# An encoder layer's down projection: 30 of its 64 row pairs as seven products of sums of blocks

## The chip, the cores and the metric

The kernel runs on one core of one Trainium2 chip. The metric is device microseconds (us) of one execution; lower is better. TensorE (PE) multiplies, VectorE (DVE), ScalarE (ACT) and GpSimd (POOL) work elementwise, and SyncE (SP), ACT and POOL issue transfers (DMAs).

## The reference, cut to what matters

One layer with 256 tokens, 2048 channels and everything in float32: an input projection, two kinds of attention, a gated merge, an output projection, and then an MLP. The change is in the last product of the MLP, `u` (256 x 8192) times `w_down` (8192 x 2048).

```python
proj = h @ w_in                       # 256x2048 by 2048x10240: q, k, v of both attentions, gates
mixed = g_a * (oa @ w_branch_a) + g_b * (on @ w_branch_b)
x = x + rms_norm(mixed @ w_out, norm_mix_post)
h = rms_norm(x, norm_mlp_pre)
u = square(relu(h @ w_up))            # 256x2048 by 2048x8192
x = x + rms_norm(u @ w_down, norm_mlp_post)
```

## The kernel before, in words

**Precision.** TensorE takes float32 at a rounded precision (`fp32r`). Each operand is therefore split in two parts: ACT casts it to `fp32r` (hi, L116), DVE subtracts that from the original (lo, L117), and a product is three matmuls: hi by hi, hi by lo, lo by hi. Every matmul of interest has a stationary operand of 128x128 and a moving one of 128x512.

**Weights.** All weights come from HBM on SP's queue into three buffers of 1 MB (pool `wp`, tag `raw`), and from there into three buffers each of hi and lo. A load on SP waits until DVE has done with the buffer of three loads earlier, and a cast on ACT waits until TensorE has done with the hi buffer of three casts earlier.

**Stages.** Projections and attention come first. Then come the gates, the branch products and the merge, in groups 1024 columns wide (`wide_group`, L671). The output projection follows (`agroup`, L221), then the up projection (`wgroup`, L184), and last the down projection, written out at L951 to L1015. In the up projection each of 16 column groups has 4 chunks of weights. Its result goes through `u_evac` (L955) into a page `u`, 128 channels by 4 blocks by 256 tokens, and all 16 pages stay in SBUF.

**The down projection before.** A loop over 64 blocks of 128 rows of `w_down`: each loads a row block whole (128x2048), splits it, and runs 24 matmuls (`dmm`, L968): 2 token halves by 4 column blocks of 512, by 3. The eight PSUM banks hold all 8 sums for the whole stage. The hi and lo of `u` are made as they are needed (`usplit`, L939). The last 3 row blocks are ordered so that one bank after the other is finished. For each, ACT squares and sums the bank (L1003) and DVE multiplies it by the gain (L1005). Per token half, DVE then adds up the sums (L1007), POOL takes the power -0.5 (L89), four DVE instructions scale and add the residual (L1012), and SP writes 4 pieces out (L1015).

**Seven products.** The gate groups already have what the change uses. A pair of row blocks k, k+1 by 1024 columns is a 2x2 block product with the 2 token halves. The plain way (`Products.eight`, L656) is 8 block products, 24 matmuls, into 4 banks. The other way (`Products.seven`, L644) is 7 block products of sums of blocks, 21 matmuls, into banks 0 to 6. At the end of a group `combine` (L662) makes the four results of them in 5 instructions. `pair_weights` (L602) prepares the weights. For a plain pair that is one cast and one subtraction of 2048 elements. For a pair of seven it is three additions (L614 to L616), a cast and a subtraction of 1536 elements (L613, L617), and two casts and two subtractions of 1024 (L622, L623). Their results lie in a pool of five buffers, of which a pair takes four. Bank 7 and banks 1 to 3 also take the plain pairs, so both kinds add up in the same group (`MIXED`, L728).

**Order.** The program's instructions are put in order per engine when it is built, by a scheduler that follows its own timeline; at run time each engine takes its instructions strictly in that order. Each transfer on SP or ACT also takes one of eight completion counters by turns, and waits until the transfer that had the counter before it is done.

Of the kernel before, what the change touches and what calls it, by code (L numbers as in the profile page):

```python
# [17 lines left out]
P = 128  # L18
# [20 lines left out]
def encoder_layer(ctx: ExitStack, tc: tile.TileContext, a, out):  # L39
# [897 lines left out]
    ust = {}  # L937

    def usplit(i):  # L939
        uh = page([P, 4, T], F32R, f"uh{i}")  # L940
        ul = page([P, 4, T], F32R, f"ul{i}")
        nc.scalar.copy(uh, uT[i])
        nc.vector.tensor_sub(ul, uT[i], uh.bitcast(F32))
        ust[i] = (uh, ul)

    def dweight(k):
        if k % 4 == 0 and k // 4 not in ust:
            usplit(k // 4)
        return weight(a["w_down"], k, 1, 0, D, f"d{k}")

    uT = []  # L951
    for cg in range(DFF // 512):
# [8 lines left out]
        uT.append(u)  # L961
        if cg == DFF // 512 - 2:
            usplit(0)

    acc = [[bank(f"acc{t}{c}", t * 4 + c >= 8 - NMM) for c in range(4)] for t in range(2)]
    NK = DFF // P
    LAST = 3
    def dmm(k, t, c, w):  # L968
        uh, ul = ust[k // 4]
        ts_ = slice(t * P, (t + 1) * P)  # L970
        cs = slice(c * 512, (c + 1) * 512)
        hi, lo = w
        nc.tensor.matmul(acc[t][c], uh[:, k % 4, ts_], hi[:, 0, cs], start=(k == 0), stop=False)  # L973
        nc.tensor.matmul(acc[t][c], uh[:, k % 4, ts_], lo[:, 0, cs], start=False, stop=False)  # L974
        nc.tensor.matmul(  # L975
            acc[t][c], ul[:, k % 4, ts_], hi[:, 0, cs], start=False, stop=(k == NK - 1)
        )

    ws = [dweight(k) for k in range(2)]
    for t in range(2):  # L980
        for k in range(2):
            for c in range(4):
                dmm(k, t, c, ws[k])
    for k in range(2, NK - LAST):
        w = dweight(k)
        for t in range(2):
            for c in range(4):
                dmm(k, t, c, w)

# [5 lines left out]
    ws = [dweight(k) for k in range(NK - LAST, NK)]
    for t in range(2):
        ssd = small(4, f"ssd{t}")
        zw = [page([P, 1024], F32, f"zw{t}{h}") for h in range(2)]
# [70 lines left out]
```

## Time and profile before

| what | value |
|---|---|
| median of 3 runs | 1386.31 us (1385.98 to 1386.63) |
| profiled execution | 1386.53 us, of which the span of the profile is 1384.7 us |
| PE busy | 1363.7 us (98% of the span) |
| DVE busy | 851.7 us (62%) |
| ACT busy | 659.6 us (48%) |
| POOL busy | 7.9 us (1%) |
| transfers | 265.11 MB, mean 191 GB/s |
| up projection, down projection | about 700 to 1027 us, 1027 to 1376 us of the span |

A row of a group of instructions has line, engine, operation, output and inputs with their shapes, the count, then busy time, mean ns of one, and the idle time of the engine just before them with what ended it. Rows of the timeline begin with the start and the duration in us. Rows of a table of windows have the window, its length, then busy us and count of PE, of weight loads (PEld), DVE, ACT and POOL, the clock that TensorE was granted, the share of the transfer engines' time, and GB/s.

### The profile page before, as it was taken

Reading aid. Unit: us, or ns where it says so; the run is one execution under the profiler, and the core shown is the slowest. Engines: PE = TensorE matmul, PEld = TensorE weight load, DVE = VectorE, ACT = ScalarE, POOL = GpSimd, SP = SyncE. Lnnn points to the kernel's source line nnn. Section 1 sums busy time; section 2 is a strip of 40 time slices with the busy share of each in tenths; the row PEclk is TensorE's granted clock in tenths of the full one; section 3 lists DMA queues with packets and bytes.
Section 4 is the critical chain, followed back from the end, with each engine's and each line's share of the span. In section 5 each row is a group of like instructions: output and inputs, shape, how many; then the busy total and the mean of one; then the engine's idle time right before and its main releaser. Section 6 shows DMA issues by size and latency. Waiting matters only on the chain.

```text
span 1384.7 us, 16956 instructions
## 1 busy us (share of the span) xinstructions
PE 1363.7 (98%) x6861; PEld 1157.6 (84%) x6861; DVE 851.7 (62%) x1093; ACT 659.6 (48%) x923; POOL 7.9 (1%) x19
## 2 busy tenths in 40 slices
PE   7999999999999999999899999999999999999997
PEld 6888888888888888888788888888888888888886
DVE  6878866677857876654755554555566554444445
ACT  7455455544643544443754444444465443333332
POOL 0000000000000000000000000000000000000000
PEclk9999999999999999999999999999999999999999
DMA  8675745564655565766456565556555556555551
GB/s 292 204 230 165 205 153 182 178 180 156 206 187 184 208 223 172 248 225 195 127 178 212 161 205 184 196 189 192 182 183 208 186 191 235 183 196 199 186 200 71
DMA packets 105198, 265.11 MB, mean 191 GB/s; under 512 B 15008, under 2 KB 16288, under 8 KB 96928
## 3 DMA queue, kind: packets, MB, share of 16 engines
q1 hardware_dynamic: 104976, 264.03, 58.2%
q8 instruction: 53, 0.87, 0.3%
q14 instruction: 25, 0.20, 0.0%
q10 hardware_dynamic: 144, 0.01, 0.0%
HBM read 261.92 MB, written 3.92 MB: 192 GB/s over the span
## 4 chain that ended last, share of the span: by engine, by line
PE 98%; DVE 1%; DMA 0%; ACT 0%; SPq 0%; issue 0%; DVEq 0%; POOLq 0%; POOL 0%; ACTq 0%
PE u_p L192 17%; PE u_p L193 9%; PE acc L975 8%; PE acc L974 8%; PE acc L973 8%; PE qa_p L192 2%; PE ka_p L192 2%; PE qn_p L192 2%; PE kn_p L192 2%; PE ga L639 2%; PE y_p L232 2%; PE y_p L231 2%; PE ga L642 2%; PE ga L641 2%; PE y_p L230 2%; PE gb L642 2%
## 5 line engine op out<-in xcount | busy, mean ns | idle before, releaser
L192 PE MATMUL u_p<-h2T,u_h 128*128 128x512 f32 x1024 | 359.3, 397 | 1.0 <-DVE h2T L870 1.0
L193 PE MATMUL u_p<-h2T,u_l 128*128 128x256 f32 x1024 | 284.1, 280 | 0.0
L117 DVE TENSOR_TENSOR d_l<-d_w,d_h 128x1024 fp32r<-128x1024 f32 x128 | 151.1, 1222 | 164.1 <-ACT d_h L116 163.7
L117 DVE TENSOR_TENSOR u_l<-u_w,u_h 128x1024 fp32r<-128x1024 f32 x128 | 151.1, 1222 | 145.1 <-ACT u_h L116 143.8
L192 PEld LDWEIGHTS u_p<-h2T,u_h 128*128 128x128 f32 x1024 | 191.7, 188 | 45.7 <-DVE h2T L870 1.2
L116 ACT CAST d_h<-d_w 128x1024 fp32r<-128x1024 f32 x128 | 127.9, 1047 | 191.5 <-PE acc L975 187.9
L974 PE MATMUL acc<-d_l,uh 128*128 128x512 f32 x512 | 199.0, 389 | 0.0
L975 PE MATMUL acc<-d_h,ul 128*128 128x512 f32 x512 | 198.9, 389 | 0.0
L973 PE MATMUL acc<-d_h,uh 128*128 128x512 f32 x512 | 198.2, 389 | 0.0
L193 PEld LDWEIGHTS u_p<-h2T,u_l 128*128 128x128 f32 x1024 | 193.5, 189 | 1.3
L116 ACT CAST u_h<-u_w 128x1024 fp32r<-128x1024 f32 x128 | 128.0, 1048 | 123.1 <-PE u_p L192 62.3
L974 PEld LDWEIGHTS acc<-d_l,uh 128*128 128x128 f32 x512 | 96.1, 188 | 20.1
L973 PEld LDWEIGHTS acc<-d_h,uh 128*128 128x128 f32 x512 | 96.1, 188 | 19.9
L975 PEld LDWEIGHTS acc<-d_h,ul 128*128 128x128 f32 x512 | 96.1, 188 | 19.8
L117 DVE TENSOR_TENSOR y_l<-y_w,y_h 128x1024 fp32r<-128x1024 f32 x32 | 37.9, 1222 | 30.9 <-ACT y_h L116 30.9
L116 ACT CAST y_h<-y_w 128x1024 fp32r<-128x1024 f32 x32 | 32.0, 1047 | 40.9 <-PE y_p L232 32.6
L230 PE MATMUL y_p<-y_h,mh 128*128 128x512 f32 x128 | 50.1, 391 | 0.0
L231 PE MATMUL y_p<-y_l,mh 128*128 128x512 f32 x128 | 49.9, 390 | 0.0
L232 PE MATMUL y_p<-y_h,ml 128*128 128x512 f32 x128 | 49.8, 390 | 0.0
L192 PE MATMUL qa_p<-hT,qa_h 128*128 128x512 f32 x128 | 47.7, 419 | 1.2 <-DVE hT L275 1.2
L192 PE MATMUL qn_p<-hT,qn_h 128*128 128x512 f32 x128 | 45.9, 400 | 0.0
L192 PE MATMUL kn_p<-hT,kn_h 128*128 128x512 f32 x128 | 45.4, 398 | 0.0
(549 smaller groups left out, 2378.3 us busy)
## 6 DMA issues: line engine op xcount, KB each, us to landing
u_w<-in_w_up SPq DMA_DIRECT2D x64, 1024.0 KB, 5.4
d_w<-in_w_down SPq DMA_DIRECT2D x64, 1024.0 KB, 5.0
y_w<-in_w_out SPq DMA_DIRECT2D x16, 1024.0 KB, 5.3
ka_w<-in_w_in SPq DMA_DIRECT2D x8, 1024.0 KB, 6.7
va_w<-in_w_in SPq DMA_DIRECT2D x8, 1024.0 KB, 5.2
qn_w<-in_w_in SPq DMA_DIRECT2D x8, 1024.0 KB, 5.1
kn_w<-in_w_in SPq DMA_DIRECT2D x8, 1024.0 KB, 5.1
vn_w<-in_w_in SPq DMA_DIRECT2D x8, 1024.0 KB, 5.1
```

The source lines that it names most:

```text
L116: nc.scalar.copy(hi[part], raw[part])
L117: nc.vector.tensor_sub(lo[part], raw[part], hi[part].bitcast(F32))
L192: nc.tensor.matmul(ps[b], hi[:, k % 4, cs], mv, start=(k == 0), stop=False)
L193: nc.tensor.matmul(ps[b][:, :T], lo[:, k % 4, cs], mv[:, :T], start=False, stop=(k == nk - 1))
L230: nc.tensor.matmul(ps[t], sh, hi[:, k % 4], start=(k == 0), stop=False)
L231: nc.tensor.matmul(ps[t], sh, lo[:, k % 4], start=False, stop=False)
L232: nc.tensor.matmul(ps[t], sl, hi[:, k % 4], start=False, stop=(k == nk - 1))
L639: nc.tensor.matmul(self.ps[i], sh, wh[:, blk], start=i not in self.begun, stop=False)
L642: nc.tensor.matmul(self.ps[i], sl, wh[:, blk], start=False, stop=last)
L973: nc.tensor.matmul(acc[t][c], uh[:, k % 4, ts_], hi[:, 0, cs], start=(k == 0), stop=False)
L974: nc.tensor.matmul(acc[t][c], uh[:, k % 4, ts_], lo[:, 0, cs], start=False, stop=False)
L975: nc.tensor.matmul(acc[t][c], ul[:, k % 4, ts_], hi[:, 0, cs], start=False, stop=(k == NK - 1))
```

## The change: what it does

The down projection becomes two halves of 1024 output columns (`g`), each a group like those of the gates with all eight banks. A half runs through 32 pairs of row blocks. A column group of the up projection (`cg`) gives 4 row blocks, that is 2 pairs, and two groups (an even one and the odd one after it) make a block of 4 pairs. The pairs of even groups are done by seven products, those of odd groups plainly, alternating. In the first block of each half three of the four are plain. So there are 15 pairs of seven and 17 plain ones in each half. Weights come as 256 rows by 1024 columns, again 1 MB each, 64 in all.

The two halves need the parts of `u` twice, in another form than before, and SBUF doesn't hold them all. So `act_sets` makes them at the end of each up group: for an even group the sums of blocks on DVE (4 instructions of 256 elements), and hi and lo of blocks and sums; for an odd group hi and lo. POOL's queue writes them to HBM (48 transfers of 0.4 to 0.5 MB: four for an even group, two for an odd one). `act_again` reads them back on ACT's queue, one block ahead, six transfers per block. The block of groups 12 and 13 stays in SBUF for the first half, that of 14 and 15 for the start of the second. `usplit` is gone.

The end changes too. Before, a bank was squared and multiplied straight from PSUM. Now the four results of a half are made by `combine` and four additions (`down_piece`). The gain of the first half is multiplied in block 6 of the second.

```diff
-    for k in range(2, NK - LAST):
-        w = dweight(k)
-        for t in range(2):
-            for c in range(4):
-                dmm(k, t, c, w)
...
+    def act_sets(cg, u):
...
+            nc.vector.tensor_sub(sums[:, 0], a21, a22)
+            nc.vector.tensor_sub(sums[:, 1], a11, a21)
+            nc.vector.tensor_sub(sums[:, 2], sums[:, 0], a11)
+            nc.vector.tensor_add(sums[:, 3], a12, sums[:, 2])
...
+            for at, src in pieces:
+                nc.scalar.copy(hi[:, at], src)
+                nc.vector.tensor_sub(lo[:, at], src, hi[:, at].bitcast(F32))
+            for n, part in (("h", hi), ("l", lo)):
...
+                nc.gpsimd.dma_start(kd, part.bitcast(F32))
...
+    def act_again(cg, g):
...
+                t = page(shape, F32R, f"b{n}{g}{cg}{i}")
+                nc.scalar.dma_start(t.bitcast(F32), kd)
...
+    def down_piece(g, t, half, ps):
+        z = zw[g, t][:, half]
+        nc.vector.tensor_add(z, z, ps)
+        sq = page([P, 512], F32, f"jd{g}{t}{half}")
+        c = g * 2 + half
+        nc.scalar.activation(sq, z, AF.Square, accum_out=ssd[t][:, c : c + 1])
+        if g:
+            gain(g, t, half)
...
+    blocks = [[NG - 4] + list(range(0, NG - 4, 2)) + [NG - 2], [NG - 2] + list(range(0, NG - 2, 2))]
+    for g in range(2):
+        pr = Products(f"p{g}", (1, 2, 3, 7))
+        for bi, b in enumerate(blocks[g]):
+            if bi == 0:
+                steps = [(b + 1, 0, 0), (b, 1, 0), (b, 0, 1), (b + 1, 1, 0)]
+            else:
+                steps = [(b, 0, 1), (b + 1, 0, 0), (b, 1, 1), (b + 1, 1, 0)]
+            end = bi == len(blocks[g]) - 1
+            for n, (cg, j, seven) in enumerate(steps):
+                w = pair_weights(wd[:, :, cg, j, g * 1024 : (g + 1) * 1024], f"d{g}{cg}{j}", seven)
...
+                            sets[g, blocks[g][bi + 1] + c] = act_again(blocks[g][bi + 1] + c, g)
...
+                if seven:
+                    pr.seven(partial(dstat7, sets[g, cg], j), w, end and n == 2)
+                    if end and n == 2:
...
+                        pr.combine([zw[g, t] for t in range(2)])
+                    continue
+                last = end and n == 3
+                for which in range(4):
+                    pr.eight(partial(dstat8, sets[g, cg], cg, j), w, which, last)
+                    if last:
+                        bank_, t, half = PLAIN[which]
+                        down_piece(g, t, half, pr.ps[bank_])
+                        if g and which % 2:
+                            finish(which // 2)
```

Three places in the instruction order matter below. In the names, `d061` is the pair of half 0, group 6, first or second pair 1; `r` is its raw weights, `h` and `l` its parts, `t` a sum of blocks and `eh`, `el` the parts of that; `bh`, `bl` are parts of `u` read back, `keep` where they lay.

First, DVE in the middle of the down projection. Before, it splits weights, and `u` now and then:

```order
L117 TENSOR_TENSOR d_l<-d_w,d_h 128x1024 x6
L943 TENSOR_TENSOR ul_9921<-u_7458,uh_9920 128x1024
L117 TENSOR_TENSOR d_l<-d_w,d_h 128x1024 x2
L943 TENSOR_TENSOR ul_10053<-u_7647,uh_10052 128x1024
L117 TENSOR_TENSOR d_l<-d_w,d_h 128x1024 x6
```

After, at the same place, from the last part of pair 061 to the plain pair 090:

```order
L623 TENSOR_TENSOR d061el_9554<-d061t_9543,d061eh_9553 128x1024
L610 TENSOR_TENSOR d071l<-d071r,d071h 128x2048
L614 TENSOR_TENSOR d080t_9612<-d080r 128x1024
L617 TENSOR_TENSOR d080l<-d080r,d080h 128x1536
L615 TENSOR_TENSOR d080t_9613<-d080t_9612,d080r 128x512
L623 TENSOR_TENSOR d080el_9620<-d080t_9612,d080eh_9619 128x1024
L616 TENSOR_TENSOR d080t_9613<-d080t_9613,d080r 128x512
L614 TENSOR_TENSOR d081t_9694<-d081r 128x1024
L610 TENSOR_TENSOR d090l<-d090r,d090h 128x2048
```

Where two subtractions served a row block, 14 instructions now serve a block of four pairs, and the first sum of 081, which needs that pair's weights from HBM, stands ahead of the subtraction of 090, which TensorE uses earlier.

Second, ACT at the same place. Before, it only casts:

```order
L942 CAST uh_9392<-u_6702 128x1024
L116 CAST d_h<-d_w 128x1024 x6
L942 CAST uh_9524<-u_6891 128x1024
L942 CAST uh_9656<-u_7080 128x1024
L116 CAST d_h<-d_w 128x1024 x8
```

After, in the block of groups 6 and 7:

```order
L613 CAST d060h<-d060r 128x1536
L622 CAST d060eh_9467<-d060t_9460 128x1024
L987 DMA bh_9475<-keeph_7404 128x768
L987 DMA bl_9477<-keepl_7406 128x768
L987 DMA bh_9479<-keeph_7412 128x1024
L987 DMA bl_9481<-keepl_7414 128x1024
L987 DMA bh_9483<-keeph_7609 128x1024
L987 DMA bl_9485<-keepl_7611 128x1024
L609 CAST d070h<-d070r 128x2048
L613 CAST d061h<-d061r 128x1536
L622 CAST d060eh_9471<-d060t_9461 128x1024
```

The six reads for the next block stand between the casts of a pair of seven.

Third, DVE at the end of the program. Before (`rd_m` goes to POOL for the power, `acc` are banks):

```order
L1005 TENSOR_TENSOR zw_10710<-acc_8600,gp_10616 128x512
L1012 SCALAR_TENSOR_TENSOR zw_10645<-zw_10645,rd_r,x_0_4833 128x512 x2
L1012 SCALAR_TENSOR_TENSOR zw_10646<-zw_10646,rd_r,x_1_4834 128x512 x2
L1005 TENSOR_TENSOR zw_10710<-acc_8601,gp_10616 128x512
L1005 TENSOR_TENSOR zw_10711<-acc_8602,gp_10617 128x512
L1005 TENSOR_TENSOR zw_10711<-acc_8603,gp_10617 128x512
L1007 TENSOR_REDUCE sd_10760<-ssd_10709 128x1
L86 TENSOR_SCALAR rd_m<-sd_10760 128x1
L1012 SCALAR_TENSOR_TENSOR zw_10710<-zw_10710,rd_r,x_2_4835 128x512 x2
L1012 SCALAR_TENSOR_TENSOR zw_10711<-zw_10711,rd_r,x_3_4836 128x512 x2
```

After, the last 13 rows but the very last, a scaling like the one before it (`p` are banks; ahead of them stand the four additions of `combine` with two of `down_piece` and one gain):

```order
L1029 TENSOR_TENSOR zw_11252<-zw_11252,p_10074 128x512
L1029 TENSOR_TENSOR zw_11252<-zw_11252,p_10078 128x512
L1025 TENSOR_TENSOR zw_11251<-zw_11251,gp_10861 128x512
L1038 TENSOR_REDUCE sd_11284<-ssd_8848 128x1
L1025 TENSOR_TENSOR zw_11252<-zw_11252,gp_10861 128x512
L86 TENSOR_SCALAR rd_m<-sd_11284 128x1
L1025 TENSOR_TENSOR zw_11252<-zw_11252,gp_10861 128x512
L1038 TENSOR_REDUCE sd_11318<-ssd_8849 128x1
L1043 SCALAR_TENSOR_TENSOR zw_10022<-zw_10022,rd_r,x_0_4833 128x512 x2
L1043 SCALAR_TENSOR_TENSOR zw_11251<-zw_11251,rd_r,x_1_4834 128x512 x2
L86 TENSOR_SCALAR rd_m<-sd_11318 128x1
L1043 SCALAR_TENSOR_TENSOR zw_10023<-zw_10023,rd_r,x_2_4835 128x512 x2
```

Before, the first token half was scaled while banks of the second were still filling. Now the additions from the last two banks stand ahead of the scaling of both halves.

More of the change, by code (lines that the diff above doesn't have):

```diff
@@ L936, in encoder_layer @@
     )
[L937 to L952, printed above, removed]
+    NG = DFF // 512
+    FIRST = (NG - 4, NG - 2)
@@ L953, in encoder_layer @@
+    def act_again(cg, g):
+        out = []
+        for i in range(2 if seven_of(cg) else 1):
+            got = []
+            for n in "hl":
+                shape, kd = kept[cg, i, n]
+                t = page(shape, F32R, f"b{n}{g}{cg}{i}")
+                nc.scalar.dma_start(t.bitcast(F32), kd)
+                got.append(t)
+            out.append(got)
+        return out
+    sets = {}
+    for cg in range(NG):
         u = page([P, 4, T], F32, f"u{cg}")
@@ L960, in encoder_layer @@
         wgroup(a["w_up"], cg * 512, lambda k: hT2[k // 2][:, k % 2], KD, u_evac, f"u{cg}", **({} if cg else first_up))
[L961 to L977, printed above, removed]
@@ L995, in encoder_layer @@
[L995 to L998, printed above, removed]
-        for c in range(4):
-            for i in range(LAST):
-                dmm(NK - LAST + i, t, c, ws[i])
-            j = junk512("jd").rearrange("p a b -> p (a b)")
-            nc.scalar.activation(j, acc[t][c], AF.Square, accum_out=ssd[:, c : c + 1])
-            cs = slice((c % 2) * 512, (c % 2 + 1) * 512)
-            nc.vector.tensor_mul(zw[c // 2][:, cs], acc[t][c], gp2[c // 2][:, cs])
+        got = act_sets(cg, u)
@@ new lines, in encoder_layer, with dstat7, dstat8 @@
+        if NG - 4 <= cg < NG - 2:
+            sets[0, cg] = got
+    temps.close()
+    mid = ctx.enter_context(tc.tile_pool(name="mid2", bufs=5, reuse_waits="tile"))
+    wd = a["w_down"].rearrange("(g h j p) c -> p h g j c", h=2, j=2, p=P)
+    def dstat7(sets, j, n):
+        part, at = (0, n) if n < 3 else (1, n - 3)
+        return tuple(p[:, at, j] for p in sets[part])
+    def dstat8(sets, cg, j, k, t):
+        if seven_of(cg):
+            return tuple(p[:, ((0, 3), (1, 2))[k][t], j] for p in sets[0])
+        return tuple(p[:, j + 2 * k, t * P : (t + 1) * P] for p in sets[0])
@@ new lines, in encoder_layer, with gain @@
+    zw = {}
+    ssd = [small(4, f"ssd{t}") for t in range(2)]
+    def gain(g, t, half):
+        z = zw[g, t][:, half]
+        nc.vector.tensor_mul(z, z, gp2[g][:, half * 512 : (half + 1) * 512])
+    def down_piece(g, t, half, ps):
+        z = zw[g, t][:, half]
+        nc.vector.tensor_add(z, z, ps)
[4 more added lines that the diff above has]
+            gain(g, t, half)
@@ L1006, in encoder_layer, with finish @@
+    def finish(t):
         sd = small(1, f"sd{t}")
-        nc.vector.tensor_reduce(sd, ssd, axis=AX.X, op=ALU.add)
+        nc.vector.tensor_reduce(sd, ssd[t], axis=AX.X, op=ALU.add)
         rd = inv_rms(sd, D, f"rd{t}")
```

50 lines of the change are left out of this document (39 added, 11 removed).

## The prediction, written before the changed kernel was run

> **What bounds the kernel now.** First the page: its busy times, and the chain of work that ended last.
>
> ```profile
> span 1384.7 us, 16956 instructions
> ...
> PE 1363.7 (98%) x6861; PEld 1157.6 (84%) x6861; DVE 851.7 (62%) x1093; ACT 659.6 (48%) x923; POOL 7.9 (1%) x19
> ...
> PE 98%; DVE 1%; DMA 0%; ACT 0%; SPq 0%; issue 0%; DVEq 0%; POOLq 0%; POOL 0%; ACTq 0%
> ```
>
> The chain is TensorE's work almost throughout. The next question is whether this holds in the two stages that the change touches. The table of windows has them (up projection, down projection) and, for later, a stretch of the gate groups with pairs of seven:
>
> ```profile
> 440.00:500.00 60.00, 60.00 (x267) 49.69 (x266) 52.96 (x50) 31.27 (x25) 0.00 (x0) 1.00 0.60 206
> 700.00:1027.00 327.00, 327.00 (x1872) 285.06 (x1871) 182.44 (x236) 156.99 (x235) 0.00 (x0) 1.00 0.58 187
> ```
> ```profile
> 1026.00:1376.00 350.00, 349.95 (x1547) 289.59 (x1545) 173.85 (x159) 144.56 (x159) 0.54 (x1) 1.00 0.55 186
> ```
>
> TensorE never pauses in either, at a granted clock of 1.00, while DVE is busy for half of the time. Only fewer matmuls, or a shorter end, can save time. What a matmul costs is read from the starts of the first and the last hi-by-hi matmul, not from the 389 ns of one, since they overlap:
>
> ```profile
> L973 PE MATMUL acc<-d_h,uh x512: 389/389/398, 1027.6 to 1375.1; 128*128 128x512 f32 x171
> ```
>
> Every third matmul is on this line, so 3 x 511 = 1533 steps took 347.5 us: 0.2267 us each.
>
> **Matmuls removed.** Thirty pairs lose 3 of 24 matmuls: 90 of 1536 go, 90 x 0.2267 = 20.4 us. All of it is on the chain. Whether it is saved depends on the feeding, which gets heavier.
>
> **Feeding one block of four pairs.** A block (seven, plain, seven, plain) is 90 matmuls, 20.4 us. The gate groups have rows for each new operation:
>
> ```profile
> L623 DVE TENSOR_TENSOR gb_3el<-gb_3t,gb_3eh 128x1024 fp32r<-128x1024 f32 x4 | 4.9, 1222 | 0.8 <-PE gb L641 0.8
> ...
> L610 DVE TENSOR_TENSOR gb_2l<-gb_2r,gb_2h 128x2048 fp32r<-128x2048 f32 x2 | 4.6, 2292 | 0.0
> ...
> L617 DVE TENSOR_TENSOR gb_3l<-gb_3r,gb_3h 128x1536 fp32r<-128x1536 f32 x2 | 3.5, 1758 | 1.4 <-ACT gb_3h L613 1.4
> ...
> L614 DVE TENSOR_TENSOR gb_3t<-gb_3r 128x1024 f32<-128x1024 f32 x2 | 2.4, 1220 | 0.0
> ```
> ```profile
> 485.94 0.69 DVE L615 TENSOR_TENSOR gb_3t<-gb_3t,gb_3r 128x512 f32<-128x512 f32 x1
> ```
> ```profile
> L622 ACT CAST gb_3eh<-gb_3t 128x1024 fp32r<-128x1024 f32 x4 | 4.2, 1048 | 0.1
> ...
> L609 ACT CAST gb_2h<-gb_2r 128x2048 fp32r<-128x2048 f32 x2 | 3.8, 1908 | 0.5 <-PE ga L642 0.5
> ...
> L613 ACT CAST gb_3h<-gb_3r 128x1536 fp32r<-128x1536 f32 x2 | 3.0, 1484 | 3.7 <-PE gb L642 2.4 <-issue 1.3
> ```
> ```profile
> L606 SPq DMA_DIRECT2D gb_2r<-in_w_in x2: 367/368/368, 344.1 to 472.3; - x2
> ```
>
> DVE: 2 x 1.22 + 4 x 0.69 + 2 x 1.76 + 4 x 1.22 + 2 x 2.29 = 18.2 us, 89% of the block. ACT: 2 x 1.48 + 4 x 1.05 + 2 x 1.91 + 6 issues of 0.37 (SP's price) = 13.2 us. The gate stretch above had DVE busy 52.96 of 60.00 us, 88%, and TensorE never paused, so the share alone is no bar.
>
> Transfers: 4 loads of 1.05 MB, and 2.88 MB read back (1.84 MB for an even group, 1.05 for an odd one), 7.08 MB. What the engines can move is seen at the start of the kernel, where loads queue up:
>
> ```profile
> 8.00:20.00 12.00, 10.81 (x47) 9.15 (x48) 8.32 (x14) 11.90 (x27) 0.00 (x0) 1.00 1.04 389
> ```
> ```profile
> d_w<-in_w_down SPq DMA_DIRECT2D x64, 1024.0 KB, 5.0
> ...
> first_w<-in_w_in SPq DMA_DIRECT2D x2, 1024.0 KB, 10.7
> ```
>
> At 389 GB/s a block's bytes take 18.2 us of 20.4. So three resources stand at 89 to 100%, and what counts is the margin of each hand-over. The tightest path runs through the first order excerpt of DVE. `d061el_9554` takes a buffer that TensorE leaves with the 49th matmul of the block, 11.1 us after its start. `d090l` is first read by the 22nd matmul of the next block, at 20.4 + 21 x 0.2267 = 25.2 us. Between lie 14.1 us. DVE's nine rows take 1.22 + 2.29 + 1.22 + 1.76 + 0.69 + 1.22 + 0.69 + 1.22 + 2.29 = 12.6 us: margin 1.5. The other way goes through HBM: once `d071l` is done (3.5 us), its buffer is free, 081 is loaded, and its first sum stands ahead of `d090l`: 3.5 + 5.0 + 1.22 + 2.29 = 12.0 us: margin 2.1. So the load of a pair like 081 may take 7.1 us from issue to landing. ACT's six issues (2.2 us) delay the cast of 070 behind them, whose margin is that of `d090l` too. [...]
>
> No row shows a load beside reads on a second queue. [...]
>
> **The up projection** gets, per even group, four sums of 256 elements and three subtractions on DVE:
>
> ```profile
> L257 DVE TENSOR_TENSOR up_s<-u_p,up_r 128x256 f32<-128x256 f32 x60 | 23.9, 419 | 0.2 <-ACT up_r L255 0.2
> ```
> ```profile
> 858.35 4.85 DVE L117 TENSOR_TENSOR u_l<-u_w,u_h 128x1024 fp32r<-128x1024 f32 x4 [5.56 <-ACT u_h L116]
> ```
>
> That is 5 x 0.42 + 0.69 + 1.22 = 4.0 us, and it stands after the group's results, where DVE waits 5.56 us for ACT, which itself waits for TensorE to free a buffer. An odd group adds 1.22. Cost 0; without that cover 8 x 4.0 + 8 x 1.22 = 42 us. The writes, 23.6 MB in 327 us, raise the rate from 187 to 259 GB/s, and POOL has nothing else to do. `usplit` goes from the down projection; it was hidden.
>
> **The start of the down projection.** ACT reaches its reads about 5.6 us after the last matmul of the up projection: cast 1.48, DVE's subtraction 1.76, its two operations of 0.42, square 0.42, cast 1.05. Then 2.88 MB come in beside the last 1.05 MB being written: 10.1 us at 389 GB/s, and 5.0 - 1.05/0.389 = 2.3 us of latency, so 18.0 us. Behind these reads ACT has the cast `d000eh` (1.05), used at the 87th matmul, at 19.5 us. It just fits; with two weight loads in between it is 5.4 us late. Cost 0 to 5.4, I take 1, since the weights of the first pairs are in by then.
>
> **The change of halves.** The second half's first matmul waits until DVE has added bank 1, behind two steps of `combine`, which wait for bank 5, done 8 matmuls (1.8 us) before the half's end. Three steps of 0.68 (row below) leave 0.3 us of pause; if the subtraction of 2.29 ahead of them is late too, 2.5. I take 1.3.
>
> **The end.** The timeline of the last 9 us, and a row of `combine`:
>
> ```profile
> 1375.56 0.39 PE L975 MATMUL acc<-d_h,ul 128*128 128x512 f32 x1
> 1376.04 0.60 ACT L1003 ACTIVATE jd<-acc 128x512 f32<-128x512 f32 x1 [1.41 <-PE acc L975]
> ...
> 1376.76 0.69 DVE L1005 TENSOR_TENSOR zw<-acc,gp 128x512 f32<-128x512 f32 x1 [1.41 <-ACT jd L1003]
> 1377.37 0.15 DVE L1007 TENSOR_REDUCE sd<-ssd 128x1 f32<-128x4 f32 x1
> 1377.55 0.15 DVE L86 TENSOR_SCALAR rd_m<-sd 128x1 f32<-128x1 f32 x1
> 1377.85 0.54 POOL L89 TENSOR_TENSOR rd_r<-rd_m,expo 128x1 f32<-128x1 f32 x1 [6.70 <-DVE rd_m L86]
> 1378.43 2.74 DVE L1012 SCALAR_TENSOR_TENSOR zw<-zw,rd_r,x 128x512 f32<-128x512 f32 x4 [0.72 <-POOL rd_r L89]
> ```
> ```profile
> 472.14 0.68 DVE L666 TENSOR_TENSOR ga<-ga,ga 128x512 f32<-128x512 f32 x1
> ```
>
> Before: the last matmul ends at 1375.95, the span 8.75 us later, of which 1384.7 - (1378.43 + 2.74) = 3.53 lie behind the last DVE instruction. After, bank 5 is ready 9 matmuls (2.0 us) before the end. From there DVE has four steps of `combine`, two additions and a gain, 7 x 0.68 = 4.8, to 2.8 us behind the end. Then come the rows of the third excerpt: two additions (1.4), three gains (2.0), two sums and a scale (0.45), four scalings of the first token half (2.74), 0.15 and 0.73 for the power, four of the second half (2.74), and 3.53: in all 16.5 us. The end grows by 7.8 us, give or take 1 for steps that overlap or wait.
>
> **Sum.** -20.4 + 7.8 + 1.3 + 1 + 1 = -9.3 us: 1377.2 for the profiled execution's 1386.53 (span 1384.7), which stands 0.2 above the median of 1386.31; so 1377.0. With all unknowns at their ends this case gives 1373 to 1384.
>
> **The rivals.**
> *One, slower: the weight loads come late.* With reads on ACT's queue in front of them, loads like 081 take as long as at the start, 10.7 us instead of 7.1. That costs 3.6 us in each of 14 blocks, 50 us: 1427. For it: first_w's row. Against it: those loads stood behind 3 MB on their own queue; here SP issues 081 before ACT issues the block's reads. It decides from 7.7 us on, where 14 x 0.6 uses up the gain.
> *Two, no change: half the rate.* If such a load shares every packet, its 2.7 us of moving double, and it lands after 7.7 us: 14 x 0.6 = 8.4 us more, 1385.4. For it: bytes fill 89% of the time. Against it: only the last microsecond of that load meets the reads.
> *Three: a cheap end.* If the end grew only by one addition (0.7), 1370. Against it: the order stands as shown.
> *Not done as said:* excluded; the program has 1446 matmuls in this stage.
>
> **How the numbers follow.** Forecast 0.70, rival one 0.13, rival two 0.12, rival three 0.05. Differences under 0.2% (2.8 us) can't be told from none here. Faster: 0.70 + 0.05 + 0.01 of rival two = 0.76; same: 0.09, slower: 0.02 of rival two, with 0.13 of rival one: 0.15. The range of 8 in 10 runs from 1372, where a cheaper end begins, to 1386, which takes in rival two and leaves rival one out.
>
> **What would show it.** In the changed profile: starts of matmuls 0.2267 us apart in the down stage; TensorE's idle time there under 5 us; the span ending 15 to 18 us after the last matmul; loads of the down stage landing within 7 us; no pause in the up stage. The forecast is wrong if DVE waits for loads in every block, or if ACT is held by its reads.

## The result, and the profile after

The changed kernel takes 1378.38 us (median; 1378.19 to 1379.15), the kernel before 1386.14 beside it: a ratio of 0.9945 (95% interval 0.9933 to 0.9957), 7.8 us less. The forecast was 1377.0. The profiled execution took 1378.19, with a span of 1376.4, so the spans differ by 8.3 us. From the page of the kernel after, span, busy times and chain:

```profile
span 1376.4 us, 17243 instructions
...
PE 1345.8 (98%) x6771; PEld 1141.3 (83%) x6771; DVE 997.7 (72%) x1245; ACT 709.7 (52%) x939; POOL 34.3 (2%) x67
...
PE 92%; DVE 3%; DMA 3%; ACT 1%; issue 1%; ACTq 0%; POOL 0%; SPq 0%; DVEq 0%; POOLq 0%
```

The chain is no longer TensorE alone: DVE, transfers and ACT now hold some of it. Where, is seen from all the waits of TensorE in the down projection and from windows (up projection, the start of the down projection, and the blocks of the first half behind it):

```profile
PE p L639 <- ACT d000eh L622: 2.5, 1, 2.5
PE p L639 <- DVE zw L1029: 0.6, 1, 0.6
PE p L641 <- DVE d191l L610: 0.4, 1, 0.4
```
```profile
700.00:1010.00 310.00, 310.00 (x1771) 270.06 (x1770) 204.74 (x279) 167.83 (x253) 20.93 (x39) 1.00 0.75 252
```
```profile
1040.00:1060.00 20.00, 17.47 (x70) 13.81 (x69) 13.53 (x12) 7.73 (x7) 0.00 (x0) 0.91 1.03 404
```
```profile
1052.00:1190.00 138.00, 138.00 (x609) 114.31 (x608) 116.73 (x94) 72.39 (x55) 0.00 (x0) 1.00 0.86 328
```

In the up projection the new sums, casts and stores raise DVE's work, and TensorE is busy for 310.00 of 310.00 us: they cost nothing. In the blocks of the first half TensorE is busy without a break too. Most of what is lost is lost at the start, and there the granted clock is 0.91 as well. The stage's first and last rows of matmuls give its length:

```profile
1026.47 0.39 PE L639 MATMUL p<-d0130h,ah 128*128 128x512 f32 x1
```
```profile
1359.90 0.61 PE L642 MATMUL p<-d1131h,bl 128*128 128x512 f32 x2
```

The second of the last two starts one step later, at 1360.13. From 1026.47 that is 333.66 us; 1446 matmuls, 1445 steps of 0.2267, would take 327.6. So the stage has a surplus of 6.1 us. Behind it lie 1376.4 - 1360.13 = 16.27 us. Before, the first matmul of the stage started at 1027.60 and the last at 1375.56: 347.96 us for 1535 steps, no surplus, and 1384.7 - 1375.56 = 9.14 behind it. The difference of the spans is made of these:

| part | forecast | measured |
|---|---|---|
| 90 matmuls less | -20.4 | -20.4 |
| start of the down projection | +1 | +4.4 |
| change of halves | +1.3 | +0.9 |
| stray misses | +1 | +0.8 |
| end | +7.8 | +7.1 |
| all before the stage's first matmul, the up projection too | 0 | -1.1 |
| sum | -9.3 | -8.3 |

Stray misses are what the other two rows leave of the surplus of 6.1; the one wait in them is that of 0.4 us at `d191l`. The -1.1 can't be put down to the change: over the changed kernel and the experiments, which do the same work up to there, the stage's first matmul starts between 1026.5 and 1028.6, and the 1027.6 of the kernel before lies among these.

**The start.** ACT's rows of the timeline (the first of twelve reads, the 11th and the 12th, and the cast behind them), then TensorE's around the pause:

```profile
1031.11 0.34 ACTq L987 DMA_DIRECT2D bh<-keeph  x1
...
1042.39 0.33 ACTq L987 DMA_DIRECT2D bh<-keeph  x1
1047.31 0.33 ACTq L987 DMA_DIRECT2D bl<-keepl  x1
1047.68 1.99 ACT L622 CAST d000eh<-d000t 128x1024 fp32r<-128x1024 f32 x2 [6.27 <-DMA bl<-keepl]
```
```profile
1045.86 0.39 PE L642 MATMUL p<-d0120eh,al 128*128 128x512 f32 x1
1048.78 0.83 PE L639 MATMUL p<-d000eh,bh 128*128 128x512 f32 x2 [2.53 <-ACT d000eh L622]
...
1050.27 0.63 PE L641 MATMUL p<-d000l,bh 128*128 128x512 f32 x1
1050.69 0.63 PE L642 MATMUL p<-d000h,bl 128*128 128x512 f32 x1
```

ACT stood for 4.9 us between the 11th and the 12th read. The 12th needed the completion counter of the 6th, which landed at 1047.24, and the cast that TensorE needed stood behind it. From 1045.86 to 1048.78 are 2.92 us instead of 0.23: 2.7 us of pause. Then steps of 0.42 follow (1050.27 to 1050.69), not 0.23: ten steps up to 1052.76 take 3.98 instead of 2.27 us, 1.7 more. The granted clock of a window of 2 us in it is 0.50:

```profile
1050.00:1052.00 2.00, 2.00 (x7) 1.52 (x6) 0.00 (x0) 1.47 (x1) 0.00 (x0) 0.50 1.03 412
```

**The end**, in rows of DVE (the first step of `combine`, the scalings of each token half):

```profile
1358.58 0.69 DVE L666 TENSOR_TENSOR zw<-zw,p 128x512 f32<-128x512 f32 x1 [5.59 <-PE p L642]
...
1366.57 2.74 DVE L1043 SCALAR_TENSOR_TENSOR zw<-zw,rd_r,x 128x512 f32<-128x512 f32 x4 [0.39 <-POOL rd_r L89]
...
1370.10 2.74 DVE L1043 SCALAR_TENSOR_TENSOR zw<-zw,rd_r,x 128x512 f32<-128x512 f32 x4 [0.72 <-POOL rd_r L89]
```

`combine` waits 5.59 us for bank 5 and begins 1.9 us ahead of the last matmul's end (1360.5), as forecast, and from there DVE works almost without a gap. Most of its additions and multiplications start 0.60 us apart, not 0.68 as reckoned, so the end came out a little shorter than forecast.

**The loads.** From issue to landing, in the block of groups 6 and 7 (the last number is us):

```profile
d061r<-in_w_down SPq DMA_DIRECT2D x1, 1024.0 KB, 4.9
d071r<-in_w_down SPq DMA_DIRECT2D x1, 1024.0 KB, 10.9
```

Loads that meet the reads of parts of `u` take about twice the 5.0 us of before. The one that was reckoned critical, 061, is issued 1.2 us ahead of the block's first read (1107.72 and 1108.97) and takes 4.9. There are 14 such loads, one for the second pair of seven of each block but the first of a half. Twelve of them take 4.9 to 6.9 us; 001 and 101, next to the start of a half, take 9.3 and 9.7, and TensorE doesn't wait for either.

### The profile page after: what moved, and what is told of

It is laid out like the page before. It is cut to its first block, busy times and chain, and to the rows that moved or that the text cites. A ratio compares the mean times of both kernels' runs of the same rounds, so it can differ in the third digit from the quotient of the medians.

```text
span 1376.4 us, 17243 instructions
## 1 busy us (share of the span) xinstructions
PE 1345.8 (98%) x6771; PEld 1141.3 (83%) x6771; DVE 997.7 (72%) x1245; ACT 709.7 (52%) x939; POOL 34.3 (2%) x67
## 4 chain that ended last, share of the span: by engine, by line
PE 92%; DVE 3%; DMA 3%; ACT 1%; issue 1%; ACTq 0%; POOL 0%; SPq 0%; DVEq 0%; POOLq 0%
PE u_p L192 17%; PE u_p L193 9%; PE p L641 6%; PE p L642 6%; PE p L639 6%; PE qa_p L192 2%; PE ka_p L192 2%; PE qn_p L192 2%; PE kn_p L192 2%; PE ga L639 2%; PE y_p L232 2%; PE ga L641 2%; PE ga L642 2%; PE y_p L230 2%; PE y_p L231 2%; PE gb L639 2%
## 5 line engine op out<-in xcount | busy, mean ns | idle before, releaser
L192 PE MATMUL ka_p<-hT,ka_h 128*128 128x512 f32 x128 | 45.0, 398 | 0.0
L999 ACT ACTIVATE u<-up_s 128x256 f32<-128x256 f32 x64 | 24.8, 417 | 26.7 <-DVE up_s L998 26.7
L255 ACT COPY up_r<-u_p 128x256 f32<-128x256 f32 x64 | 23.6, 368 | 26.4 <-PE u_p L193 26.3
L193 PE MATMUL qn_p<-hT,qn_l 128*128 128x256 f32 x128 | 35.9, 281 | 0.0
L193 PE MATMUL kn_p<-hT,kn_l 128*128 128x256 f32 x128 | 35.7, 280 | 0.0
L193 PE MATMUL qa_p<-hT,qa_l 128*128 128x256 f32 x128 | 35.2, 285 | 0.0
L193 PE MATMUL ka_p<-hT,ka_l 128*128 128x256 f32 x128 | 35.2, 280 | 0.0
L192 PEld LDWEIGHTS qa_p<-hT,qa_h 128*128 128x128 f32 x128 | 24.9, 197 | 6.7 <-DVE hT L275 1.6
```

The source lines that it names most:

```text
L192: nc.tensor.matmul(ps[b], hi[:, k % 4, cs], mv, start=(k == 0), stop=False)
L193: nc.tensor.matmul(ps[b][:, :T], lo[:, k % 4, cs], mv[:, :T], start=False, stop=(k == nk - 1))
L255: nc.scalar.copy(r, ps[:, T:])
L999: nc.scalar.activation(u[:, b], s, AF.Square)
```

## The experiments

All times are medians of four or more executions, compared with the kernel before on the same chip (there it took 1386.0 to 1386.6). The table has the stage as above, worked out in the same way for each: first and last start of a matmul, the surplus over steps of 0.2267 us, and what lies from the last start to the end of the span.

| kernel | time | first | last | surplus | behind |
|---|---|---|---|---|---|
| before | 1386.14 | 1027.60 | 1375.56 | 0.0 | 9.1 |
| after | 1378.38 | 1026.47 | 1360.13 | 6.1 | 16.3 |
| reads after casts | 1374.75 | 1028.39 | 1357.63 | 1.7 | 16.5 |
| last pair in order | 1372.87 | 1027.23 | 1358.18 | 3.4 | 12.6 |
| both | 1370.96 | 1026.82 | 1355.63 | 1.2 | 12.5 |
| 28 pairs plain | 1419.03 | 1027.23 | 1406.43 | 32.6 | 12.5 |
| 28 plain, reads held | 1388.38 | 1027.62 | 1374.28 | 0.0 | 12.5 |
| reads on SP | 1376.71 | 1028.12 | 1358.56 | 2.9 | 16.4 |
| 1 MB more ahead of critical loads | 1425.48 | 1026.48 | 1408.62 | 54.6 | 16.1 |
| no reads | 1369.92 | 1027.81 | 1355.37 | 0.0 | 12.6 |
| 0.5 MB more | 1397.67 | 1028.61 | 1380.44 | 24.3 | 16.3 |
| both ends in order | 1372.22 | 1027.34 | 1358.76 | 3.8 | 12.5 |
| gains on POOL | 1373.99 | 1027.59 | 1357.41 | 2.2 | 13.4 |
| reads ahead on SP | 1373.42 | 1027.34 | 1355.20 | 0.3 | 16.1 |

**1. The reads behind the casts.**

```diff
-            nc.scalar.copy(h2[i], t[i])
+            last_cast[0] = nc.scalar.copy(h2[i], t[i]).ins
...
-                            sets[g, blocks[g][bi + 1] + c] = act_again(blocks[g][bi + 1] + c, g)
+                            with tc.issue_after(last_cast[0]) if bi == 1 else nullcontext():
+                                sets[g, blocks[g][bi + 1] + c] = act_again(blocks[g][bi + 1] + c, g)
```

> Only the six reads for the second following block (groups 2 and 3 of the first half, and their like in the second half) are moved: ACT issues them behind the two casts of sums of the first pair of seven of the block before (d000eh, d100eh) instead of ahead of them. Theory (the pause of 2.7 us at the start of the down projection, and the 1.7 us that the matmuls at half clock behind it cost, come from ACT standing at its 11th and 12th read with the cast d000eh behind it): both go, 1378.4 - 4.4 = 1374.0 us. Rival (the transfers' rate is what is short there: two blocks' reads and five weight loads in 25 us): the pause moves to another wait of about the same size, 1377 to 1379 us.

Measured: 1374.75 (ratio to before 0.9918, 0.9904 to 0.9933). The one wait of TensorE that is left in the stage:

```profile
PE p L641 <- DVE zw L1031: 0.6, 1, 0.6
```

Pause and half clock at the start are gone; the surplus falls from 6.1 to 1.7, by the 4.4 us expected. The profiled execution is only 2.3 us shorter, since its stage began 1.9 later; the median falls by 3.6. The rival's transfers were not what was short: the loads of 010 and 001 take 9.8 and 9.0 us here, 10.3 and 9.3 in the changed kernel, and TensorE doesn't wait for them.

**2. The last pair in order.**

```diff
-            nc.tensor.matmul(self.ps[i], sl, wh[:, blk], start=False, stop=last)
+            self.newest = nc.tensor.matmul(self.ps[i], sl, wh[:, blk], start=False, stop=last).ins
...
-                    pr.eight(partial(dstat8, sets[g, cg], cg, j), w, which, last)
+                    with tc.issue_after(pr.newest) if last and g else nullcontext():
+                        pr.eight(partial(dstat8, sets[g, cg], cg, j), w, which, last)
```

> Only the end: the 24 matmuls of the very last plain pair stand behind all those of the last pair of seven, instead of between them. Theory (the end is 7.1 us longer than before because combine waits for bank 5, done 9 matmuls before the end): combine's four additions go before the end. Behind the last matmul are left an addition 0.6, two gains 1.2, sum and scale 0.2, four scalings 2.74, power 0.73 and 0.15, four scalings 2.74 and the 3.53 behind the last DVE instruction: 11.9 us instead of 15.9, so 1378.4 - 4.0 = 1374.4. Rival: TensorE then waits for the last part of pair 1121, which DVE ends at 1353.0 and the matmuls in this order want at about 1352.4: 0.6 to 1 us of it comes back as a pause, and more if the half clock follows: 1375 to 1377.

Measured: 1372.87 (0.9906, 0.9889 to 0.9922). The first step of `combine`, TensorE's last matmul and the last scalings:

```profile
1352.78 0.69 DVE L666 TENSOR_TENSOR zw<-zw,p 128x512 f32<-128x512 f32 x1 [1.76 <-PE p L642]
...
1358.18 0.39 PE L642 MATMUL p<-d1131h,bl 128*128 128x512 f32 x1
...
1364.43 2.74 DVE L1043 SCALAR_TENSOR_TENSOR zw<-zw,rd_r,x 128x512 f32<-128x512 f32 x4 [0.72 <-POOL rd_r L89]
```

`combine` now begins 5.8 us ahead of the last matmul's end, not 1.9, and the end shrinks from 16.3 to 12.6 us: the theory's 11.9 behind the matmul's end, within 0.4. TensorE did not wait for pair 1121. The other 1.5 us of the gain were not expected: the pause at the start was 1.4 us here instead of 2.5, and no half clock came behind it. That makes the surplus 2.7 us lower, of which 0.8 is lost again because the stage began later.

**3. Both.** The two diffs above together.

> Both edits, of the reads at the start and of the last pair. Theory: they lie at different ends of the stage and add up, 1378.4 - 4.4 - 4.0 = 1370.0 us. Rival: one of the two gains nothing, 1374.

Measured: 1370.96 (0.9891, 0.9876 to 0.9905). They add up: surplus 1.2, 12.5 behind. This is the fastest kernel of the study but for one that leaves work out, 15 us under the kernel before; of the 20.4 us of matmuls only the longer end (3.3) and 1.2 are paid back.

**4. 28 pairs plain.**

```diff
-            return tuple(p[:, ((0, 3), (1, 2))[k][t], j] for p in sets[0])
+            return tuple(p[:, ((0, 3 if cg in FIRST else 2), (1, 2))[k][t], j] for p in sets[0])
...
-                steps = [(b + 1, 0, 0), (b, 1, 0), (b, 0, 1), (b + 1, 1, 0)]
+                steps = [(b + 1, 0, 0), (b, 1, 0), (b, 0, 0), (b + 1, 1, 0)]
...
-                steps = [(b, 0, 1), (b + 1, 0, 0), (b, 1, 1), (b + 1, 1, 0)]
+                end_ = bi == len(blocks[g]) - 1
+                steps = [(b, 0, 0), (b + 1, 0, 0), (b, 1, int(end_)), (b + 1, 1, 0)]
```

> 28 of the 30 pairs of seven are done plainly: only the last pair of seven of each half stays, so combine, the end and the layout of loads, stores and reads stay as they are. In the plain pairs of even groups, except those of the first block, the fourth block of u is replaced by the second of the last two that are at hand, which changes numbers and no time. Theory (each pair of seven saves its 3 matmuls in full, since the feeding is hidden): 28 x 3 x 0.2267 = 19.0 us more, 1397.4, less up to 4.4 us if the pause at the start goes with the cast d000eh: 1393.0 to 1397.4. Rival (the heavier feeding of the pairs of seven costs several us in the blocks that the waits don't show): less than 1391.

Measured: 1419.03 (1.0239, 1.0223 to 1.0254), far from both. TensorE's longest wait, and ACT's ahead of it:

```profile
PE p L639 <- ACT d001h L609: 11.6, 1, 11.6
```
```profile
ACT d001h L609 <- DMA bl<-keepl: 20.1, 1, 20.1
```

ACT issues the reads of several blocks in a row at the start of each half, ahead of the casts. Plain pairs take no pages of SBUF for sums of blocks, and free pages are probably what let the scheduler do so; no run shows that. It is the mechanism of experiment 1, made larger by accident; for the price of a matmul the run says nothing.

**5. 28 pairs plain, reads held.** As 4, with the edit of 1 for every block (and with `last_cast` set by the casts of plain pairs too).

> The run with 28 pairs done plainly once more, and now ACT issues each block's six reads only behind the cast of the first pair of the block before, so that they can't gather at the start of a half (the same numbers of u are replaced). Theory (3 matmuls saved per pair of seven, in full): the run with the reads held back, 1374.75, plus 28 x 3 x 0.2267 = 19.0: 1393.8, give or take 2. Rival (the feeding of pairs of seven costs several us that no wait shows): under 1391. If reads still stand ahead of casts at the start, pauses there show and are taken off.

Measured: 1388.38 (1.0015, 1.0006 to 1.0025), 13.6 more than run 1. By the time alone the rival won (under 1391). The stage's first and last matmul say otherwise:

```profile
1027.62 0.39 PE L641 MATMUL p<-d0130h,ah 128*128 128x512 f32 x1
```
```profile
1374.28 0.39 PE L644 MATMUL p<-d1131h,bl 128*128 128x512 f32 x1
```

1529 steps took 346.66 us, 0.2267 each: every matmul costs its full step. Against run 1 the stage is 17.4 longer, that is 84 x 0.2267 = 19.0 less the 1.7 of surplus that run 1 has. The end is 4.0 shorter, because in this program the last plain pair stands behind the last pair of seven of itself. Steps of the same length in both kinds of pair mean that each pair of seven saves its three matmuls. The feeding of the pairs of seven costs at most the surplus of run 1, 1.7 us in all, in that order.

**6. The reads on SP's queue.**

```diff
-                nc.scalar.dma_start(t.bitcast(F32), kd)
+                nc.sync.dma_start(t.bitcast(F32), kd)
```

> All reads of parts of u go to SP's queue, in program order among the weight loads: twelve of them (5.8 MB) ahead of d010 at the start, and six right behind each load like that of 061 and ahead of the one like 071. Theory (what counts in a block is that loads like 061 land within 7.1 us, and that other loads have several us more): no cost in the blocks, since the reads stand behind those loads; at the start ACT is free of reads, but the loads of 010 and 001 wait behind 5.8 MB, 14 us at 411 GB/s, so a pause of some us remains there: 1376 to 1380. Rival (taking turns between two queues is what lets the weights through): loads behind 2.9 MB of reads land 7 us later in every block, and 14 blocks lose 1 to 4 us each, 1392 or more.

Measured: 1376.71 (0.993, 0.9915 to 0.9945), as the theory had it; TensorE's only waits are 0.6 and 1.1 us for 010, at the start. The loads of the same block:

```profile
d061r<-in_w_down SPq DMA_DIRECT2D x1, 1024.0 KB, 5.1
d071r<-in_w_down SPq DMA_DIRECT2D x1, 1024.0 KB, 10.6
```

Behind the reads on one queue a load takes what it takes beside them on another (10.6 and 10.9). Two queues with work share the engines: in the changed kernel, from 1117 to 1121, SP's queue moves 204 packets, 0.84 MB, in 52.1% of the engines' time, and ACT's 203 packets, 0.77 MB, in 47.9%. The landings agree: there, with two queues, 071 is issued 1.6 us behind the last of the six reads (1112.91 and 1111.28) and lands 0.4 ahead of it (1123.80 and 1124.19). In this run, with one queue, it lands 3.5 us behind the last read (1120.99 and 1117.52). The order of the two landings is the same in ten blocks of each kernel.

**7. and 9. More bytes ahead of the critical loads**, 1 MB (7) and 0.5 MB (9, one load instead of two).

```diff
+                for m in range(2 if bi and n == 2 else 0):
+                    more = nc.sync.dma_start(page([P, 1024], F32, ...), a["w_up"][...]).ins
+                with tc.issue_after(more) if more else nullcontext():
+                    w = pair_weights(...)
```

> 1 MB more per block: two unused loads of 0.5 MB each stand on SP's queue right ahead of each load like that of 061 (the second pair of seven of a block), which then lands about 2.6 us later, at 7.7 to 8 us. Theory (the tightest path has 2.1 us to spare through HBM): 14 x 0.6 = 8 us more, 1386, with DVE seen waiting for these loads; less if the changed order on DVE puts the subtraction of the plain pair ahead of the sum. Rival (the margin is larger than reckoned, as loads of 8 to 12 us elsewhere in the block cost nothing): no change, 1378.

> As the run with 1 MB more per block, with one unused load of 0.5 MB ahead of each critical load instead of two. That run lost 47 us: its critical loads landed in 8.7 to 12.2 us, each with a pause of 1.5 to 4.7 us behind it. Theory (a critical load may take 7.1 us): it is issued some 1.3 us earlier now, and lands in 6.3 us where the reads don't reach it and in about 8 where they do: 0 to 1 us of pause in each of 14 blocks, and no half clock behind pauses under 1.6 us: 1379 to 1390. Rival (any byte more in a block tips it over, since the transfers are full): half of the 47 us, 1402.

Measured: 1425.48 (1.028, 1.0263 to 1.0297) and 1397.67 (1.0082, 1.0067 to 1.0097). Of run 7, the first of the two extra loads and the critical one on SP, and the wait of DVE and of TensorE for it:

```profile
1112.47 4.35 SPq L1061 DMA_DIRECT2D more<-in_w_up  x2
1122.57 0.38 SPq L606 DMA_DIRECT2D d061r<-in_w_down  x1
```
```profile
DVE d061t L614 <- DMA d061r<-in_w_down: 5.9, 1, 5.9
```
```profile
PE p L639 <- ACT d061h L613: 2.4, 1, 2.4
```

Late critical loads do stop TensorE, in ten blocks for 1.5 to 4.7 us, so "the margin is larger" has fallen for this order. The size was forecast far too small, and not for the bytes alone: SP stood for completion counters, which its loads share with ACT's reads. The second extra load went out at 1116.48, when 070 had landed (1116.42), and 061 at 1122.57, when the first of the block's reads had (1122.50). So 061 was issued 10.1 us behind the first extra load, and then it met the reads and took 8.9 us. In run 9 ten of the 14 critical loads land in 5.0 to 7.4 us and TensorE doesn't wait for them. The other four, 001, 101, 181 and 1101, take 9.4 to 11.5 us. Three of these are waited for, and the two longest waits are among them:

```profile
PE p L639 <- ACT d181h L613: 3.8, 1, 3.8
PE p L639 <- ACT d001h L613: 2.6, 1, 2.6
PE p L639 <- ACT d151h L609: 1.8, 1, 1.8
```
```profile
d181r<-in_w_down SPq DMA_DIRECT2D x1, 1024.0 KB, 11.5
```

The late critical loads make 8.3 of the 14.1 us of waits; most of the rest is for plain pairs like 151 and 071. The granted clock over 1026 to 1380 is 0.99. Run 9 cost 18 us of surplus, nearer to its rival (bytes) than to its theory, which took all critical loads to land within 8 us. Why four of them were late in run 9 is settled for 181 only: two loads of the gain, which stand behind it in the changed kernel, stand ahead of it on SP, and it waited for the counter of a read (landed at 1310.54, 181 issued at 1310.55). Both edits move instructions on DVE as well.

**8. No reads.**

```diff
-                            sets[g, blocks[g][bi + 1] + c] = act_again(blocks[g][bi + 1] + c, g)
+                            sets[g, blocks[g][bi + 1] + c] = sets[g, b + c]
```

> Nothing is read back: every block takes the parts of u of the half's first block, so the sums are of other numbers; the matmuls, the weights' loads and their preparation stay. Theory (reads cost something only at the start): 1378.4 - 4.4 - 0.4 = 1373.6, as in the run with the reads held back (1374.75), with weight loads landing in about 5 us. Rival (the reads cost in every block, through late weights or ACT's time for issuing them): 1370 or less.

Measured: 1369.92 (0.988, 0.9865 to 0.9895), in the rival's range, but for another reason. The window over the stage:

```profile
1026.00:1355.00 329.00, 329.00 (x1456) 272.50 (x1455) 279.48 (x242) 173.09 (x143) 1.06 (x2) 1.00 0.58 199
```

No surplus, 1.7 less than run 1; and an end of 12.6, because here too the last pair came to stand in order. Of the 8.5 us under the changed kernel 3.7 are the end, and 6.1 the surplus, which went with the reads and with the order that came of leaving them out (the first matmul came 1.3 later); 4.4 of the 6.1 are the start, as in run 1.

**10. Both ends in order; 11. three gains on POOL.** Run 10 changes run 3 by the first edit, run 11 by both.

```diff
-                    with tc.issue_after(pr.newest) if last and g else nullcontext():
+                    with tc.issue_after(pr.newest) if last else nullcontext():
...
-        nc.vector.tensor_mul(z, z, gp2[g][:, half * 512 : (half + 1) * 512])
+        eng = nc.gpsimd if g and (t, half) != (1, 0) else nc.vector
+        eng.tensor_mul(z, z, gp2[g][:, half * 512 : (half + 1) * 512])
```

> The run with both edits (1370.96), and the last plain pair in order behind the last pair of seven in the first half too. Theory: the pause of 0.6 to 0.8 us at the change of halves goes, since bank 5 is then done 24 matmuls ahead of it: 1370.2. Rival: the subtraction of the second half's first weights stands between combine's steps on DVE and keeps the pause: no change, 1371.

> As the run before, and three of the four gains of the second half are multiplied on POOL, which is idle there. Theory (behind the last matmul DVE is the bound: in the run with the last pair in order it has no gap of over 0.8 us between its first combine step and its last scaling): two gains of 0.6 us leave the path, 1.2 us less, and up to 2 if the power is ready earlier: 1368.2 to 1369. Rival (a multiplication of 128x512 on POOL takes several us, or slows DVE beside it): the scalings wait for it, 1371 or more.

Measured: 1372.22 (0.99, 0.9885 to 0.9915) and 1373.99 (0.9914, 0.9898 to 0.9931); neither helps over run 3. In run 10 the order of the first half's end has a new wait, and half clock behind it (steps of 0.43 us; the granted clock over 1180 to 1200 is 0.91); in run 11 POOL's multiplications and DVE's beside them:

```profile
1187.02 0.50 PE L643 MATMUL p<-d0141el,bh 128*128 128x512 f32 x1 [1.78 <-DVE d0141el L625]
...
1188.42 0.63 PE L643 MATMUL p<-d0151l,bh 128*128 128x512 f32 x1
1188.85 0.63 PE L644 MATMUL p<-d0151h,bl 128*128 128x512 f32 x1
```
```profile
1356.11 2.53 POOL L1028 TENSOR_TENSOR zw<-zw,gp 128x512 f32<-128x512 f32 x2 [320.75 <-ACT jd L1035]
...
1357.84 0.69 DVE L1032 TENSOR_TENSOR zw<-zw,p 128x512 f32<-128x512 f32 x1 [0.42 <-PE p L644]
...
1359.13 1.25 POOL L1028 TENSOR_TENSOR zw<-zw,gp 128x512 f32<-128x512 f32 x1
1359.31 1.62 DVE L1028 TENSOR_TENSOR zw<-zw,gp 128x512 f32<-128x512 f32 x1 [0.79 <-ACT jd L1035]
```

At the change of halves DVE has loads of the next half to split, and the plain matmuls that the scheduler had put between those of seven covered that: the same edit that saves 3.7 us at the end costs a pause of 1.8 here. Both theories fell. In run 11 the step that failed is that DVE is the bound: ahead of its last addition it waits 0.42 us for TensorE, and ahead of its one multiplication 0.79 for ACT's square of the same piece, so two gains less on DVE had nothing to win. On POOL a multiplication takes 1.27 us, and the one on DVE that runs beside it 1.62 instead of 0.69; the end grows by 0.9.

**12. The reads ahead of the critical load, on SP.**

```diff
-                nc.scalar.dma_start(t.bitcast(F32), kd)
+                newest[0] = nc.sync.dma_start(t.bitcast(F32), kd).ins
...
-                if n == 0:
+                early = n == (2 if bi else 0)
+                if early:
...
+                with tc.issue_after(newest[0]) if early and bi and not end else nullcontext():
+                    w = pair_weights(...)
```

> As the run with all reads on SP's queue (1376.71), but the six reads of a block now stand ahead of the critical load (061 and its like) instead of behind it; no byte is added. Theory (a critical load is late only if it meets the reads in time): in the changed kernel SP issues 070 7.6 us ahead of 061; 2.88 MB at 411 GB/s take 7.0 us, so the reads are nearly through when 061 starts, it lands in 5 to 7.5 us, and a block loses 0 to 0.5 us: 1376 to 1384. Rival one of the prediction (a critical load behind the reads on a queue lands in 10.7 us or more): 12 us, 4.9 us late in each of 14 blocks, 69 us and the half clock behind each pause: 1445 or more.

Measured: 1373.42 (0.9905, 0.9889 to 0.9922), and no wait of TensorE in the stage at all. The critical load, its place on SP behind the last read, and DVE ahead of it:

```profile
d061r<-in_w_down SPq DMA_DIRECT2D x1, 1024.0 KB, 11.0
```
```profile
1101.18 0.40 SPq L989 DMA_DIRECT2D bl<-keepl  x1
1101.68 0.42 SPq L606 DMA_DIRECT2D d061r<-in_w_down  x1
```
```profile
1099.02 2.29 DVE L610 TENSOR_TENSOR d051l<-d051r,d051h 128x2048 fp32r<-128x2048 f32 x1
1101.22 1.22 DVE L623 TENSOR_TENSOR d041el<-d041t,d041eh 128x1024 fp32r<-128x1024 f32 x1
```

The load takes 11.0 us, as the rival said, and costs nothing. That the blocks lose nothing is as the theory had it, but its reason is not right: the reads were not through. The time is also 2.6 us under the theory's range, because the pauses of run 6 at the start went as well: eight reads stand ahead of the load of 010 now, not twelve. What changed in the blocks is DVE's order. In the changed kernel the rows are the other way round:

```profile
1104.27 1.22 DVE L623 TENSOR_TENSOR d041el<-d041t,d041eh 128x1024 fp32r<-128x1024 f32 x1 [3.08 <-ACT d051h L609]
1105.41 2.29 DVE L610 TENSOR_TENSOR d051l<-d051r,d051h 128x2048 fp32r<-128x2048 f32 x1
```

There `d041el` waits for a buffer of TensorE (free with a matmul of pair 040 that ends at 1104.16; the row names a cast of ACT that ends 0.04 later and that `d041el` doesn't read), and the subtraction of 051, which frees the raw buffer that 061 takes, stands behind it: 061 is issued at 1107.72 and lands at 1112.6. In run 12 it is issued at 1101.68 and lands at 1112.7. This order with the last pair of run 2 was not tried; by the sum, an estimate, it would take 1373.4 - 3.7 = 1369.7.

## Why the prediction was right, and where it was not

- **90 matmuls, -20.4: right.** Runs 5, 8 and 12 have steps of 0.2267 us with a surplus of 0.3 us at most, with few pairs of seven and with all; run 12 keeps every read too.
- **Feeding a block: right in its result.** TensorE waits in the 14 blocks behind the start but once, for 0.4 us (`d191l`). That the path named was the tightest is not shown. Run 7 shows that it breaks when the critical load lands late. Run 12 shows that its first link matters, the wait of a second sum's part for TensorE ahead of the subtraction that frees the buffer: without it a load of 11.0 us costs nothing. "The load of a pair like 081 may take 7.1 us from issue to landing" is no sharp bound. The 8.7 us and more of ten loads of run 7 did cost waits, but 7.4 us (121, run 9) and 8.7 (021, run 1) cost none, nor did the 9.3 and 9.7 of 001 and 101 in the changed kernel. The forecast that loads of the stage land within 7 us was wrong: many take 8 to 12. Most of the critical ones are issued clear of the reads. The 1 us that the sum takes for stray misses is a term that no run shows; the runs showed 0.8 in its place, with that one wait of 0.4.
- **The up projection, 0: right**, by TensorE's 310.00 of 310.00 us.
- **The start, 1 taken out of 0 to 5.4: the term that was mis-sized, 4.4.** The step was that ACT has the cast `d000eh` behind "these reads", 2.88 MB, and that it just fits. The order has twelve reads ahead of it, those of two blocks. So ACT stood at the last of them, the pause was 2.7, and 1.7 more came from the half clock, which the prediction did not reckon with. Run 1 shows both gone with that order alone. That 4.4 lies under the upper end of 5.4 is luck: the 5.4 is the time of two weight loads, without the half microsecond by which the cast was reckoned to fit. One of the prediction's signs of being wrong, that ACT is held by its reads, did show, but here alone.
- **Change of halves, 1.3: about right**, 0.9. `combine` has bank 5 at 1193.24; the subtraction of 1141, ahead of it on DVE, ends at 1193.70; three steps later TensorE goes on, at 1195.68. It is the three steps of the forecast and a fifth of its 2.29 for the subtraction.
- **The end, 7.8: right**, 7.1, by the steps given; run 2 shows that it hangs on when bank 5 is done.
- **The sum, -9.3 against -8.3, is closer than its parts.** The start is 3.4 us worse than forecast; the end, the change of halves and the stray misses are 1.3 better, and 1.1 is the scatter of where the stage begins.
- **Rival one** (late loads, 50 us): late critical loads are as dear as it says, but reads on ACT's queue don't make them late. That run 7 pays 47 us is partly luck: about 32 of it are waits more than in the changed kernel, in ten blocks and not 14, and most of the rest is half clock (steps of 0.42 to 0.43 us behind six of the waits), which the rival left out. **Rival two** (half rate): loads beside reads do slow down, to 8 to 12 us, but in twelve of 14 blocks not the critical ones. **Rival three** (cheap end): excluded as the order stands; run 2 goes half the way.

## What to carry to other kernels

A fraction of work saved on a bound engine is saved in full when each hand-over keeps its margin, as in run 12 with its surplus of 0.3 us. What is lost here is lost at the seams, where the steady pattern begins, changes and ends. So cost the first block, the last and the change between two parts from their own order, and count every transfer that stands ahead of a needed instruction, those of the block after next too.

How long a load takes is no price by itself (11.0 us cost nothing in run 12): look for the instruction that frees its buffer, and whether that stands behind one that waits for the bound engine. A transfer more can also cost through the counter that it takes and not through its bytes: in run 7 the critical load 061 went out when a counter came free, 10.1 us behind the first extra load.

Where a scheduler changes the order elsewhere too, read a run part by part (first and last matmul, surplus, end). Its time alone can speak for the wrong theory, as in runs 5 and 8.

## What the runs showed of the hardware

- **Half clock behind a short pause.** Behind TensorE's wait of 2.5 us in the changed kernel the granted clock was 0.50 for 3.4 us (1049.3 to 1052.7). All single waits of the down projection from 2.5 us up, in the changed kernel and in runs 4 and 7, had such a stretch behind them, of 3.4 us or a multiple. Of eight single waits from 1.1 to 2.4 us in runs 2, 6, 7, 10 and 11 only one had it, of 1.8 us (run 10), besides two of 1.3 and 1.8 us in run 4 with 0.5 us between them. The others had none, among them one of 1.8 (run 11) and two of 2.4 (run 7; a window behind one of them is below), so the length alone doesn't decide; what else does, no run shows. Waits of 2.5 us, and once 1.8, were enough.

```profile
1133.00:1137.00 4.00, 3.52 (x13) 2.33 (x14) 4.00 (x5) 3.86 (x5) 0.00 (x0) 1.00 0.63 201
```

- **The rate of the transfers.** With loads and reads queued, the 20 us of the start above had 404 GB/s and a window of 2 us in it 422, above the 389 that the prediction took:

```profile
1042.00:1044.00 2.00, 2.00 (x10) 1.68 (x9) 2.00 (x3) 0.00 (x0) 0.00 (x0) 1.00 1.03 422
```

- **POOL beside DVE.** In run 11 a multiplication of two SBUF operands on DVE takes 1.62 us instead of 0.69 beside one on POOL. DVE's additions, which read one operand from a bank, keep their 0.69 beside POOL's other two (the row of 1357.84). With three of the four gains on POOL the end is 13.4 us, against 12.5 in run 10. Why the one operation is slowed and the others are not, no run shows.
